# Transposed attention weights gathered into full PSUM banks, and the attention units in another order

## The chip, the cores and the metric

The kernel runs on one core of one Trainium2 chip. The metric is the device time of one execution in microseconds (us); less is better. A figure "of the profile" comes from one execution that was recorded by the hardware profiler. PE is TensorE, ACT ScalarE, DVE VectorE, POOL GpSimd, and SP the engine that issues most of the DMAs.

## What is computed

One encoder layer over 2048 tokens of width 1024, in float32. The mixer has 16 heads of width 64: eight of stick-breaking attention and eight of chunked softmax attention. Cut to what matters here:

```python
mod = silu(c) @ w_ada + b_ada                      # shifts, scales, gates
proj = (rmsnorm(x, g_norm1) * (1 + sc1) + sh1) @ w_in
q_sb, k_sb, v_sb, q_ca, k_ca, v_ca = split(proj)
# stick-breaking: strictly causal
z = q @ k.T * scale
w = where(strict, exp(log_sigmoid(z) + suffix_sum(log_sigmoid(-z))), 0)
o_sb = w @ v
# chunked: own chunk of 64 and 8 before it, learned bias by clipped distance
q, k = rmsnorm(q_ca, g_q), rmsnorm(k_ca, g_k)
o_ca = softmax(q @ k.T * scale + bias) @ v
x = x + gt1 * (concat(o_sb, o_ca) @ w_o)
h = rmsnorm(x, g_norm2) * (1 + sc2) + sh2
x = x + gt2 * (square(relu(h @ w1)) @ w2)
```

## The kernel before

Everything is kept transposed (features on partitions, tokens along the free axis) and the token order is reversed, so that a causal query block looks at key blocks with the same or a higher number. The tokens are cut into NTB = 4 blocks of TB = 512. Products of float32 are made of two parts: `split` (line 138) writes a rounded high part with an ACT copy and the rest as a low part with a DVE subtraction, and a product takes two or three matmuls of these parts.

There are three stages. First come the norm and most of the input projection. Then, from about 420 us of the profile, the attention stage, which the change concerns. Last come the output projection of one token block, the second norm and the MLP, in dense matmuls.

**Units and steps.** The attention stage works through a list `units` (line 1071). A unit is one head, one query block g and, for a stick-breaking unit (class SB, line 756), one key block c; a chunked-softmax unit (class CA, line 820) takes the key blocks g and g + 1 together, and for g = 3 only block 3. There are 80 SB units, 32 of them diagonal (c = g), and 32 CA units. Each unit has STEPS = 4 steps, one for each 128 queries. Step i of the main loop (from line 1149) is the front step of one unit and the back step of the unit LAG = 8 steps, so two units, earlier.

- Front of an SB step: `scores` puts q·k in a PSUM bank `z` (issued one step ahead); `soft1` applies a sigmoid on ACT, a multiplicative scan along the keys on DVE (tile `p`) and a difference on POOL (tile `b`, the weights).
- Front of a CA step: `scores` into `cz` (and, at the unit's first step, the last 128 keys of all four steps into one bank `ct`); `soft1` adds the bias and takes the minimum on DVE; `soft2` makes the exponential on ACT (tile `e`); a DVE reciprocal and a POOL product that scale it follow one step later, in the list `first`.
- Back of a step, in the list `js`: `transposes` (line 727) turns 128x128 blocks of the weights on PE into a PSUM bank `wt`; `parts` (line 735) splits that bank into `wth` (ACT) and `wtl` (DVE); `values` (line 745) multiplies both with the value rows into the accumulator `acc`, at most AVLAG = 3 pieces later.

The piece in which this is done is a key block kb of 128 keys with the queries q0 to q1 that see it. A diagonal SB unit has 4 pieces of 512, 384, 256 and 128 columns. A CA unit with g < 3 has 8 pieces, of 512, 512, 384, 256, 128, 384, 256 and 128 columns, two in each step; with g = 3 it has the 4 of the diagonal. All other SB units have 4 pieces of 512.

**What sets the order.** `z`, `cz`, `ct` and `wt` all come from one pool of 4 PSUM banks (`pz`, line 95) in turn, so PE can begin a new one only when the engines have done with the one four before it. PE keeps program order. Between steps, `fill` (line 1086) adds dense matmuls from a list `filler`: first the remaining input projections (`fill_qkv`, line 949, tiles `pf`), then output projections (`outproj`, line 1000, tiles `po`). A step earns credit in proportion to its unit's weight, one credit pays one matmul of 512 columns, and unspent credit is cut to CAP = 5. After a finished bank of the filler, fill rests until the next step, and at the start of a filler for some steps:

```python
        RESTS = {"wait": 4, "start": 3}
```

An output projection of block g is appended to `filler` when its last pair of heads has been stored (`keep`, line 707): there it is the last CA pair.

ACT holds one set of function tables. The sigmoid of the SB units and the exponential of the CA units stand in different ones, and the compiled program has an ACT_TABLE_LOAD wherever the front goes over from one kind of head to the other. The order of the units before was

```python
        for h in range(NH):
            units += [SB(h, 2, 2), SB(h, 2, 3), SB(h, 3, 3)]
        units += [CA(h, g) for h in range(NH) for g in (2, 3)]
        for g in (1, 0):
            units += [SB(h, g, c) for h in range(NH) for c in range(g, NTB)]
            units += [CA(h, g) for h in range(NH)]
```

so the kind of head changes five times: before units 24, 40, 64, 72 and 104.

Of the kernel before, what the change touches and what calls it, by code (L numbers as in the profile page):

```python
# [18 lines left out]
P = 128  # L19
# [3 lines left out]
NH = 8  # L23
# [56 lines left out]
def encoder_kernel(ctx, tc, xT, c, g1, g2, w_in, w_rest, gqk, bias, w_o, w1, w2, w_ada, b_ada, out):  # L80
# [567 lines left out]
    if True:  # L648
# [67 lines left out]
        pend = {}  # L716

        class Unit:
# [8 lines left out]
            def transposes(self, j):  # L727
                kb, q0, q1 = self.blocks[j]
                nm = f"{self.nm}_{kb}"
                wt = pz.tile([P, TB], F32, tag="z", name=f"wt{nm}")  # L730
                for qi in range(q0, q1):
                    pe.transpose(wt[:, qi * P : (qi + 1) * P], self.weights(qi, kb), ident)
                self.wt[j] = wt

            def parts(self, j):
                kb, q0, q1 = self.blocks[j]
                nm = f"{self.nm}_{kb}"
                wt = self.wt[j]
                wh = wtp.tile([P, TB], F32R, tag="wth", name=f"wth{nm}")
                wl = wtp.tile([P, TB], F32R, tag="wtl", name=f"wtl{nm}")  # L740
                cols = slice(q0 * P, q1 * P)
                split(wh[:, cols], wl[:, cols], wt[:, cols])
                self.wt[j] = (wh, wl, cols, kb)

            def values(self, j):
                if j == 0 and self.first:
                    pend["acc"] = ppo.tile([P, TB], F32, tag="acc", name=f"acc{self.nm}")
                self.acc = pend["acc"]
                wh, wl, cols, kb = self.wt.pop(j)
                end = self.last and j == len(self.blocks) - 1  # L750
                pe.matmul(self.acc[:, cols], self.v[:, kb, :], wh[:, cols], start=self.first and j == 0, stop=False)
                pe.matmul(self.acc[:, cols], self.v[:, kb, :], wl[:, cols], start=False, stop=end)
                if end:
                    soon.append(lambda: finish(self))

        class SB(Unit):
            ca = 0

            def __init__(self, h, g, c):
                self.c = c  # L760
                super().__init__(h, g, c == g, c == NTB - 1)
                self.nm += f"_{c}"
                self.diag = c == g
                self.weight = 0.7 if self.diag else 1.0
                self.blocks = [(kb, 0, kb + 1 if self.diag else 4) for kb in (3, 2, 1, 0)]
# [54 lines left out]
        class CA(Unit):  # L820
            ca = 1

            def __init__(self, h, g):
# [3 lines left out]
                order = [3] + [kb for kb in (4, 2, 1, 0, 5, 6, 7) if kb < self.nk // P]  # L827
                self.blocks = [(kb, max(0, kb - 4), min(4, kb + 1)) for kb in order]
# [257 lines left out]
        def fill(part):  # L1086
# [62 lines left out]
        for i in range(len(steps) + LAG):  # L1149
# [11 lines left out]
            if back is not None:  # L1161
                nb = len(back.blocks)
# [3 lines left out]
            if front is not None:  # L1166
# [15 lines left out]
            fill(front.weight if front else 0.6)  # L1182
# [530 lines left out]
```

## Time and profile before

| | |
|---|---|
| time, median of 3 runs | 2623.31 us (2622.73 to 2624.0) |
| time of the profiled execution | 2620.22 us |
| its span, first to last instruction | 2618.2 us |
| busy: PE, DVE, ACT, POOL | 98%, 72%, 54%, 34% of the span |
| transposes of SB weights (`wt` from `b`) | 1088, from 429.5 to 1242.1 us |
| transposes of CA weights (`wt` from `e`) | 560, from 595.0 to 1317.2 us |
| casts `wth` and subtractions `wtl` | 544 each |
| ACT_TABLE_LOAD | 6, of 1283 ns each |

The table is read so: the span is what the instructions cover, and the time of the same execution is 2.0 us longer. The busy share of PE is of a pipelined engine: the time of one matmul in the profile runs over that of the next, so a busy PE may still be doing less than it could. The `wt` rows show where the attention stage lies, from about 420 to 1318 us. Nearly all rows of the profile carry line 42, since a helper records every operation; the tiles' names tell them apart.

### The profile page before, as it was taken

Reading aid. Unit: us, or ns where it says so; the run is one execution under the profiler, and the core shown is the slowest. Engines: PE = TensorE matmul, PEld = TensorE weight load, DVE = VectorE, ACT = ScalarE, POOL = GpSimd, SP = SyncE. Lnnn points to the kernel's source line nnn. Section 1 sums busy time; section 2 is a strip of 40 time slices with the busy share of each in tenths; the row PEclk is TensorE's granted clock in tenths of the full one; section 3 lists DMA queues with packets and bytes.
Section 4 is the critical chain, followed back from the end, with each engine's and each line's share of the span. In section 5 each row is a group of like instructions: output and inputs, shape, how many; then the busy total and the mean of one; then the engine's idle time right before and its main releaser. Section 6 shows DMA issues by size and latency. Waiting matters only on the chain. (4 is left out here: it accounts for less than half of the span.)

```text
span 2618.2 us, 39617 instructions
## 1 busy us (share of the span) xinstructions
PE 2565.2 (98%) x12816; PEld 2153.3 (82%) x12816; DVE 1881.5 (72%) x3222; ACT 1408.0 (54%) x2704; POOL 896.3 (34%) x1224
## 2 busy tenths in 40 slices
PE   6999999999999999999999999999999999999999
PEld 5888887888789988787888888788888888888887
DVE  7656767887789879898768787668766565555555
ACT  5333434678866676666754444556544454544443
POOL 4330144666666567666604323000002322200000
PEclk9999999999999999999999999999999999999999
DMA  9879977788787688666697777776764434375574
GB/s 344 305 302 363 333 297 252 240 260 260 248 261 226 217 276 262 222 204 209 218 340 249 259 258 277 277 273 231 258 223 173 154 139 166 125 263 195 197 271 151
DMA packets 257039, 640.20 MB, mean 245 GB/s; under 512 B 28736, under 2 KB 60480, under 8 KB 246976
## 3 DMA queue, kind: packets, MB, share of 16 engines
q1 hardware_dynamic: 255536, 632.96, 70.1%
q10 hardware_dynamic: 1296, 4.72, 0.4%
q8 instruction: 101, 1.65, 0.3%
q14 instruction: 106, 0.87, 0.1%
HBM read 446.20 MB, written 191.37 MB: 244 GB/s over the span
## 5 line engine op out<-in xcount | busy, mean ns | idle before, releaser
L42 PE MATMUL ps<-oph,opv 128*128 128x512 f32 x2688 | 614.0, 390 | 1.8 <-ACT opv L42 1.6
L42 PE MATMUL ps<-h,opw 128*128 128x512 f32 x2664 | 604.5, 389 | 0.5 <-DVE cx L42 0.5
L42 PEld LDWEIGHTS ps<-oph,opv 128*128 128x128 f32 x2688 | 505.1, 188 | 108.8 <-ACT opv L42 2.5
L42 PEld LDWEIGHTS ps<-h,opw 128*128 128x128 f32 x2664 | 500.1, 188 | 104.6 <-DVE cx L42 0.9
L42 POOL TENSOR_TENSOR b<-p 128x512 f32<-128x512 f32 (+1 forms) x320 | 291.9, 912 | 219.5 <-DVE p L42 129.6
L42 ACT CAST wth<-wt 128x512 fp32r<-128x512 f32 (+3 forms) x544 | 257.1, 483 | 191.3 <-PE wt L42 180.9
L42 DVE TENSOR_TENSOR wtl<-wt,wth 128x512 fp32r<-128x512 f32 (+3 forms) x544 | 290.6, 545 | 65.0 <-ACT wth L42 62.7
L42 DVE TENSOR_TENSOR oph<-hw,oph 128x512 fp32r<-128x512 f32 x224 | 156.0, 696 | 222.0 <-ACT oph L42 222.0
L42 ACT CAST oph<-hw 128x512 fp32r<-128x512 f32 x224 | 139.3, 622 | 284.9 <-PE ps L42 268.8
L42 PE MATMUL pt<-w,ht 128*128 128x512 f32 x1248 | 288.8, 391 | 2.2 <-DVE qh L42 2.2
L42 PEld LDWEIGHTS pt<-w,ht 128*128 128x128 f32 x1248 | 232.8, 188 | 50.6 <-ACT csq L42 2.9
L42 POOL TENSOR_TENSOR ts<-w 128x512 f32<-128x512 f32 x32 | 46.7, 1460 | 659.5 <-DMA w<-in_w_dram 570.7
L42 DVE TENSOR_TENSOR_SCAN p<-z,p,zero 128x512 f32<-128x512 f32 x192 | 245.6, 1280 | 29.8 <-ACT z L42 24.1
L42 PE MATMUL acc<-wth,v 128*128 128x512 f32 (+3 forms) x544 | 220.9, 410 | 0.2 <-DMA q<-scr_q 0.2
L42 ACT ACTIVATE z<-z 128x512 f32<-128x512 f32 (+1 forms) x320 | 166.2, 520 | 59.0 <-PE z L42 48.6
L42 PE MATMUL z<-k,q 128*128 128x512 f32 (+3 forms) x640 | 184.8, 371 | 8.4 <-DVE p L42 5.9
L42 PE MATMUL acc<-wtl,v 128*128 128x512 f32 (+3 forms) x544 | 185.6, 348 | 0.0
L42 DVE TENSOR_TENSOR opw<-w,opw 128x512 fp32r<-128x512 f32 x127 | 98.8, 780 | 113.2 <-ACT opw L42 113.1
L42 POOL TENSOR_TENSOR e<-e,cols 128x640 f32<-128x640 f32 (+4 forms) x128 | 142.9, 1121 | 104.7 <-DVE cols L42 61.8
L42 PE MATMUL wt<-ident,b 128*128 128x128 f32 x1088 | 171.3, 272 | 2.7 <-DVE cols L42 2.3
L42 PEld LDWEIGHTS wt<-ident,b 128*128 128x128 f32 x1088 | 134.3, 140 | 33.0 <-DVE cols L42 3.5
L42 PE MATMUL po<-fx,ow 128*128 128x512 f32 x576 | 160.3, 393 | 0.0
(190 smaller groups left out, 4069.5 us busy)
## 6 DMA issues: line engine op xcount, KB each, us to landing
hw<-scr_hid SPq DMA_DIRECT2D x112, 512.0 KB, 3.9
q<-scr_q SPq DMA_DIRECT2D x128, 256.0 KB, 4.7
w<-in_w_dram SPq DMA_DIRECT2D x64, 512.0 KB, 5.2
hw<-scr_s SPq DMA_DIRECT2D x64, 512.0 KB, 4.6
k<-scr_k SPq DMA_DIRECT2D x240, 128.0 KB, 4.0
v<-scr_v SPq DMA_DIRECT2D x120, 256.0 KB, 3.9
fw<-scr_w SPq DMA_DIRECT2D x28, 1024.0 KB, 6.1
wa<-in_w_ada_dram SPq DMA_DIRECT2D x48, 512.0 KB, 6.7
```

The lines of the kernel that those rows point to most:

```text
L42: return lambda *x, **y: self.tc.keep_in_program_order(f(*x, **y))
```

## The change

Three things change.

**Banks.** In place of the list of pieces, a unit has a list `banks`, and each bank holds one or two pieces (key block, first and last query, place in the bank). For a diagonal SB unit and a CA unit with g = 3 this is `DIAG`: 512, then 384 + 128, then 256 columns. A CA unit with g < 3 has 512, 512, and three banks of two pieces with 512 columns in all. `transposes` fills the whole bank, `parts` splits the whole bank at once, and `values` still makes two matmuls for each piece, with the same columns as before. So the transposes and the matmuls stay the same in number and size, and the splits go from 544 to 432: three fewer in each of 24 CA units, one fewer in each of 8 CA units with g = 3 and of 32 diagonal SB units. A unit with 3 banks does none in its first back step and one in each other; a unit with 5 does one in each and two in the last.

**Order.** The CA units of g = 1 stand right behind those of g = 2 and 3, and the SB units of g = 1 and g = 0 follow each other, so the kind of head changes three times: before units 24, 48 and 104. An output projection is now appended when all eight pairs of its block are stored, whichever comes last.

**At a change of kind.** In the first step of a unit whose kind differs from the one before (`turned`), `soft1` is issued behind the splits of that step's back unit, and `fill` is given 6 credits more.

```diff
-            if u.ca and u.h == NH - 1 and u.g > 0:
+            pairs[u.g] += 1
+            if pairs[u.g] == KT and u.g > 0:
                 filler.append(Filler(outproj, u.g))
...
             def transposes(self, j):
-                kb, q0, q1 = self.blocks[j]
-                nm = f"{self.nm}_{kb}"
+                nm = f"{self.nm}_{j}"
                 wt = pz.tile([P, TB], F32, tag="z", name=f"wt{nm}")
-                for qi in range(q0, q1):
-                    pe.transpose(wt[:, qi * P : (qi + 1) * P], self.weights(qi, kb), ident)
+                for kb, q0, q1, at in self.banks[j]:
+                    for n, qi in enumerate(range(q0, q1), at):
+                        pe.transpose(wt[:, n * P : (n + 1) * P], self.weights(qi, kb), ident)
                 self.wt[j] = wt
...
-                cols = slice(q0 * P, q1 * P)
-                split(wh[:, cols], wl[:, cols], wt[:, cols])
-                self.wt[j] = (wh, wl, cols, kb)
+                n = P * sum(q1 - q0 for _, q0, q1, _ in self.banks[j])
+                split(wh[:, :n], wl[:, :n], wt[:, :n])
+                self.wt[j] = wh, wl
...
-                pe.matmul(self.acc[:, cols], self.v[:, kb, :], wh[:, cols], start=self.first and j == 0, stop=False)
-                pe.matmul(self.acc[:, cols], self.v[:, kb, :], wl[:, cols], start=False, stop=end)
+                for m, (kb, q0, q1, at) in enumerate(self.banks[j]):
+                    mine = slice(at * P, (at + q1 - q0) * P)
+                    for l in range(2):
+                        pe.matmul(
+                            self.acc[:, q0 * P : q1 * P], self.v[:, kb, :], w[l][:, mine],
+                            start=self.first and j + m + l == 0, stop=end and l == 1 and m == len(self.banks[j]) - 1,
+                        )
...
+        DIAG = [[(3, 0, 4, 0)], [(2, 0, 3, 0), (0, 0, 1, 3)], [(1, 0, 2, 0)]]
...
-                order = [3] + [kb for kb in (4, 2, 1, 0, 5, 6, 7) if kb < self.nk // P]
-                self.blocks = [(kb, max(0, kb - 4), min(4, kb + 1)) for kb in order]
+                if self.nk == TB:
+                    self.banks = DIAG
+                else:
+                    self.banks = [[(3, 0, 4, 0)], [(4, 0, 4, 0)]]
+                    self.banks += [[(kb, 0, kb + 1, 0), (kb + 5, kb + 1, 4, kb + 1)] for kb in (2, 1, 0)]
...
-        for g in (1, 0):
-            units += [SB(h, g, c) for h in range(NH) for c in range(g, NTB)]
-            units += [CA(h, g) for h in range(NH)]
+        units += [CA(h, 1) for h in range(NH)]
+        units += [SB(h, g, c) for g in (1, 0) for h in range(NH) for c in range(g, NTB)]
+        units += [CA(h, 0) for h in range(NH)]
...
-            credit = min(credit, CAP) + part * (work - credit) / (weight * 0.95)
+            credit = min(credit, CAP) + part * (work - credit) / (weight * 0.95) + more
...
+            turned = front is not None and i and front.ca != steps[i - 1][0].ca
-            if front is not None:
+            if front is not None and not turned:
                 front.soft1(fs)
             while first:
                 first.pop(0)()
             for j in js:
                 back.parts(j)
                 late.append((back, j))
+            if turned:
+                front.soft1(fs)
...
-            fill(front.weight if front else 0.6)
+            fill(front.weight if front else 0.6, 6 if turned else 0)
```

How the instructions move is seen at three places. In the rows a name such as `wth_2_2_3` gives head, query block and then, before, the key block of the piece, and after, the number of the bank; the last number is a running one.

The first place is ACT in the CA run, in the four steps in which the unit of head 2, g = 2 is the back unit. Before, it has eight casts, two in each step, between the exponentials `e` of the front unit:

```order
L42 CAST wth_2_2_3_7074<-wt_2_2_3_7057 128x512
L42 CAST wth_2_2_4_7078<-wt_2_2_4_7062 128x512
L42 ACTIVATE e_3_2_0_7082,cols<-s_3_2_0_7067,cols 128x640
L42 CAST wth_2_2_2_7104<-wt_2_2_2_7092 128x384
L42 CAST wth_2_2_1_7108<-wt_2_2_1_7096 128x256
L42 ACTIVATE e_3_2_1_7112,cols<-s_3_2_1_7070,cols 128x640
L42 CAST svf_11_1_7114<-pf_11_1_6700 128x8x64
L42 CAST wth_2_2_0_7148<-wt_2_2_0_7137 128x128
L42 CAST wth_2_2_5_7152<-wt_2_2_5_7139 128x384
L42 ACTIVATE e_3_2_2_7156,cols<-s_3_2_2_7100,cols 128x640
```

Now, in the same place, it has five, all of 512 columns:

```order
L42 CAST wth_2_2_0_6956<-wt_2_2_0_6944 128x512
L42 ACTIVATE e_3_2_0_6960,cols<-s_3_2_0_6949,cols 128x640
L42 COPY otmp_0_2_6717<-acc_1_2_6821 64x512
L42 COPY o_0_2_6716<-acc_1_2_6821 64x512
L42 CAST wth_2_2_1_6980<-wt_2_2_1_6970 128x512
L42 ACTIVATE e_3_2_1_6984,cols<-s_3_2_1_6952,cols 128x640
L42 CAST wth_2_2_2_7015<-wt_2_2_2_7005 128x512
L42 ACTIVATE e_3_2_2_7019,cols<-s_3_2_2_6976,cols 128x640
L42 CAST wth_2_2_3_7042<-wt_2_2_3_7029 128x512
L42 CAST wth_2_2_4_7046<-wt_2_2_4_7034 128x512
L42 ACTIVATE e_3_2_3_7050,cols<-s_3_2_3_7011,cols 128x640
```

One cast stands before each of the first three exponentials, and two before the fourth.

The second place is ACT at the first change from CA to SB heads (the front goes over to head 0, g = 1, key block 1). Before, the table load and the first sigmoid stand ahead of that step's two casts:

```order
L42 ACTIVATE e_7_3_3_8278,cols<-s_7_3_3_8253,cols 128x128
L42 COPY otmp_6_2_8281<-acc_6_2_8115 64x512
L42 COPY o_6_2_8280<-acc_6_2_8115 64x512
L42 ACT_TABLE_LOAD
L42 ACTIVATE z_0_1_1_0_8287<-z_0_1_1_0_8287 128x512
L42 CAST wth_7_2_3_8312<-wt_7_2_3_8294 128x512
L42 CAST wth_7_2_4_8316<-wt_7_2_4_8299 128x512
```

Now the step's one cast stands ahead of the load:

```order
L42 ACTIVATE e_7_1_3_9181,cols<-s_7_1_3_9128,cols 128x640
L42 COPY otmp_4_1_9184<-acc_4_1_9043 64x512
L42 COPY o_4_1_9183<-acc_4_1_9043 64x512
L42 CAST wth_6_1_0_9208<-wt_6_1_0_9201 128x512
L42 ACT_TABLE_LOAD
L42 ACTIVATE z_0_1_1_0_9192<-z_0_1_1_0_9192 128x512
L42 ACTIVATE z_0_1_1_1_9222<-z_0_1_1_1_9222 128x384
```

The split of the step no longer waits for the load, and the sigmoids come behind it.

The third place is PE at the same change, from the step's last value products to the next transposes (x2 and x3 are matmuls in a row). Before:

```order
L42 MATMUL acc_6_3_8284<-wth_6_3_1_8256,v_6_2_7880 128x256
L42 MATMUL acc_6_3_8284<-wtl_6_3_1_8257,v_6_2_7880 128x256
L42 MATMUL z_0_1_1_1_8324<-k_0_1_1_8050,q_0_1_8047 128x384 x2
L42 MATMUL pf_3_1_8243<-fx_2_6696,fw_3_0_7545 128x512 x2
L42 MATMUL wt_7_2_2_8329<-ident,e_7_2_0_8078 128x128
```

Now:

```order
L42 MATMUL acc_5_1_9187<-wtl_5_1_2_9133,v_5_1_8851 128x128
L42 MATMUL z_0_1_1_1_9222<-k_0_1_1_8933,q_0_1_8930 128x384 x2
L42 MATMUL pf_1_1_9153<-fx_2_6570,fw_1_0_8555 128x512 x2
L42 MATMUL pf_1_1_9153<-fx_3_6572,fw_1_0_8555 128x512 x3
L42 MATMUL pf_1_1_9153<-fx_4_6876,fw_1_1_8678 128x512 x3
L42 MATMUL wt_6_1_1_9235<-ident,e_6_1_0_8952 128x128
```

Between the second scores of the new unit and the next transposes stand eight filler matmuls in place of two. At the change before unit 24 there are also some more; at the one before unit 104 there are none either before or now, since the filler list rests there at the start of an output projection.

More of the change, by code (lines that the diff above doesn't have):

```diff
@@ L748, in values @@
                 self.acc = pend["acc"]
-                wh, wl, cols, kb = self.wt.pop(j)
-                end = self.last and j == len(self.blocks) - 1
-                pe.matmul(self.acc[:, cols], self.v[:, kb, :], wh[:, cols], start=self.first and j == 0, stop=False)
-                pe.matmul(self.acc[:, cols], self.v[:, kb, :], wl[:, cols], start=False, stop=end)
+                w = self.wt.pop(j)
+                end = self.last and j == len(self.banks) - 1
+                for m, (kb, q0, q1, at) in enumerate(self.banks[j]):
[5 more added lines that the diff above has]
+                        )
                 if end:
                     soon.append(lambda: finish(self))
+        DIAG = [[(3, 0, 4, 0)], [(2, 0, 3, 0), (0, 0, 1, 3)], [(1, 0, 2, 0)]]
         class SB(Unit):
@@ L764, in __init__ @@
                 self.weight = 0.7 if self.diag else 1.0
-                self.blocks = [(kb, 0, kb + 1 if self.diag else 4) for kb in (3, 2, 1, 0)]
+                if self.diag:
+                    self.banks = DIAG
+                else:
+                    self.banks = [[(kb, 0, 4, 0)] for kb in (3, 2, 1, 0)]
             def load(self):
@@ L1084, in encoder_kernel, with fill @@
         late, soon, first = [], [], []
-        def fill(part):
+        def fill(part, more=0):
             nonlocal credit, rest, work, weight
-            credit = min(credit, CAP) + part * (work - credit) / (weight * 0.95)
+            credit = min(credit, CAP) + part * (work - credit) / (weight * 0.95) + more
             weight -= part
@@ L1161, in encoder_kernel @@
             if back is not None:
-                nb = len(back.blocks)
+                nb = len(back.banks)
                 js = range(nb * bs // STEPS, nb * (bs + 1) // STEPS)
```

6 lines of the change are left out of this document (4 added, 2 removed).

## The prediction

> **What bounds the kernel now.** I read the page first. Its span, its first list and one of its groups of instructions:
>
> ```profile
> span 2618.2 us, 39617 instructions
> PE 2565.2 (98%) x12816; PEld 2153.3 (82%) x12816; DVE 1881.5 (72%) x3222; ACT 1408.0 (54%) x2704; POOL 896.3 (34%) x1224
> L42 PE MATMUL ps<-h,opw 128*128 128x512 f32 x2664 | 604.5, 389 | 0.5 <-DVE cx L42 0.5
> ```
>
> PE is the bound: it is idle for 53.0 us of the span. No matmul or transpose is taken away by the change, so it can win only what PE waits inside the attention stage. The next view is busy time by windows, cut where the kind of head changes (width, then PE, weight loads, DVE, ACT, POOL, granted clock, DMA share, GB/s):
>
> ```profile
> 435.00:580.00 145.00, 142.82 (x854) 122.72 (x853) 122.47 (x180) 99.86 (x210) 95.47 (x181) 1.00 0.79 242
> 580.00:600.00 20.00, 19.25 (x139) 17.97 (x138) 15.41 (x55) 16.09 (x36) 10.31 (x10) 1.00 1.03 292
> 600.00:705.00 105.00, 99.48 (x636) 87.55 (x636) 75.69 (x285) 86.25 (x217) 66.84 (x66) 0.98 0.82 256
> 705.00:722.00 17.00, 13.44 (x74) 10.89 (x72) 9.57 (x27) 12.19 (x29) 8.70 (x15) 0.90 0.71 203
> 722.00:893.00 171.00, 170.68 (x1085) 151.73 (x1084) 155.06 (x194) 111.90 (x216) 109.69 (x192) 1.00 0.74 235
> 893.00:905.00 12.00, 11.58 (x84) 10.72 (x84) 8.88 (x33) 8.46 (x17) 5.59 (x5) 1.00 0.89 263
> 905.00:970.00 65.00, 63.83 (x419) 56.38 (x418) 50.73 (x183) 49.81 (x118) 39.13 (x32) 1.00 0.87 271
> 970.00:995.00 25.00, 23.43 (x140) 19.52 (x140) 18.98 (x34) 19.50 (x42) 15.71 (x24) 1.00 0.85 282
> 1084.00:1100.00 16.00, 13.05 (x73) 10.11 (x72) 12.34 (x17) 8.73 (x17) 10.24 (x20) 1.00 0.64 199
> 1222.00:1242.00 20.00, 17.49 (x104) 13.93 (x103) 15.09 (x49) 12.07 (x24) 11.80 (x15) 1.00 0.62 187
> 1350.00:1650.00 300.00, 300.00 (x1326) 248.38 (x1325) 242.46 (x329) 146.06 (x256) 98.94 (x62) 1.00 0.76 272
> ```
>
> Width less PE gives the idle time: 5.52 us in the run of chunked-softmax (CA) units of g = 2 and 3 (600:705), 3.56 where it ends (705:722), 0.75, 0.42 and 1.57 at the first, third and fourth change (580:600, 893:905, 970:995), 1.17 in the CA units of g = 1, 2.18 among the first stick-breaking (SB) units, 2.95 and 2.51 at 1084 and 1222. Two windows also lose clock: 0.02 of 105 is 2.1 us, 0.10 of 17 is 1.7. The last row, from the MLP where PE never rests, gives the price of a matmul of 512 columns: 300 / 1326 = 226 ns from start to start. One is shown as 389 ns long, so each wait hides another 0.16 us behind the modelled end.
>
> Then the waits of PE in the two worst windows (total, times, longest), first 600:705, then 705:722:
>
> ```profile
> PE cz L42 <- DVE wtl L42: 2.7, 2, 2.0
> PE cz L42 <- DVE cols L42: 2.1, 3, 0.9
> PE wt L42 <- DVE cols L42: 0.6, 1, 0.6
> ```
>
> ```profile
> PE wt L42 <- DVE cols L42: 2.3, 1, 2.3
> PE z L42 <- DVE cols L42: 1.2, 1, 1.2
> ```
>
> PE waits to begin a score bank or a bank of transposes, and DVE ends the wait: the pool of four PSUM banks is full, because DVE, itself behind ACT, has not read one out. Nowhere in these windows does PE wait for a load.
>
> **The change part by part.** *Fewer splits.* The casts and the subtractions by size:
>
> ```profile
> L42 ACT CAST wth<-wt 128x512 fp32r<-128x512 f32 x280 | 163.4, 587 | 122.0 <-PE wt L42 119.1 <-PE acc L42 0.3
> L42 ACT CAST wth<-wt 128x384 fp32r<-128x384 f32 x88 | 42.3, 480 | 33.7 <-PE wt L42 27.4 <-PE acc L42 6.0
> L42 ACT CAST wth<-wt 128x256 fp32r<-128x256 f32 x88 | 32.8, 373 | 15.5 <-PE wt L42 14.9
> L42 ACT CAST wth<-wt 128x128 fp32r<-128x128 f32 x88 | 23.4, 265 | 20.2 <-PE wt L42 19.5
> L42 DVE TENSOR_TENSOR wtl<-wt,wth 128x512 fp32r<-128x512 f32 x280 | 186.4, 672 | 21.8 <-ACT wth L42 20.9
> L42 DVE TENSOR_TENSOR wtl<-wt,wth 128x384 fp32r<-128x384 f32 x88 | 47.9, 544 | 12.7 <-ACT wth L42 12.5
> L42 DVE TENSOR_TENSOR wtl<-wt,wth 128x256 fp32r<-128x256 f32 x88 | 36.1, 410 | 26.0 <-ACT wth L42 25.9
> L42 DVE TENSOR_TENSOR wtl<-wt,wth 128x128 fp32r<-128x128 f32 x88 | 24.4, 277 | 4.5 <-ACT wth L42 3.3
> ```
>
> 384 + 128 columns in one go save 480 + 265 - 587 = 158 ns of ACT and 544 + 277 - 672 = 149 ns of DVE; 256 + 256 save 159 and 148. Over 112 merges that is 17.7 us of ACT and 16.6 us of DVE, most of it under PE's own work. On the path it counts where PE waits for these engines. In 600:705 there are eight pairs of CA units with four merges each: 32 x 0.158 = 5.1 us of ACT (busy 86.25 of 105), and each step but the unit's last now asks for one bank of transposes where it asked for two, out of four. PE loses 5.52 + 2.1 us there; I take 5.0 as won, with bounds of 0 (the waits sit where nothing was merged) and 7.6. In 905:970 and 435:580 the same merges stand against 1.17 + 2.18 = 3.35 us; I take 1.5 (0 to 3.35), since in the SB units only one merge in a diagonal unit helps.
>
> *Fewer changes of kind.* ACT around the second change, and what PE does then:
>
> ```profile
> 710.06 0.58 ACT L42 COPY o<-acc 64x512 f32<-64x512 f32 x1
> 710.66 1.28 ACT L42 ACT_TABLE_LOAD   x1
> 711.95 0.58 ACT L42 ACTIVATE z<-z 128x512 f32<-128x512 f32 x1
> 712.44 0.59 ACT L42 CAST wth<-wt 128x512 fp32r<-128x512 f32 x1
> ```
>
> ```profile
> 709.10 1.04 PE L42 MATMUL wt<-ident,e 128*128 128x128 f32 x8
> 710.91 0.64 PE L42 MATMUL pf<-fx,fw 128*128 128x512 f32 x2
> 713.84 0.33 PE L42 MATMUL wt<-ident,e 128*128 128x128 f32 x1 [2.29 <-DVE cols L42]
> ```
>
> The load holds ACT for 1.3 us from the copy's end to the next sigmoid, and the casts stand behind it, so no bank comes free and PE runs out of work for 2.29 us. Two of five changes go. Their windows, 893:905 and 970:995, lose 0.42 + 1.57 = 2.0 us; I take all of it (bounds 0 and 2.0). The Trainium skill, page "ScalarE: Activation LUTs", section "What ACT_TABLE_LOAD costs", puts a switch at 1283 ns and about 1380 ns of drain, 2.66 us; the trace agrees with the 1283 and shows no drain (710.64 to 710.66). By the page two removed switches would free an estimated 5.3 us and the sum below would be up to 3.3 us better; by the rows they free 2.6.
>
> *At a change.* The one remaining change from CA to SB has its cast ahead of the load, and eight filler matmuls in place of two. The chain there is cast, load, sigmoid and scan, the last from its row:
>
> ```profile
> L42 DVE TENSOR_TENSOR_SCAN p<-z,p,zero 128x512 f32<-128x512 f32 x192 | 245.6, 1280 | 29.8 <-ACT z L42 24.1 <-POOL p L42 5.0
> ```
>
> 0.59 + 1.29 + 0.58 + 1.28 = 3.7 us, against PE work of some 3.5 us by the order: value products 0.45, scores 0.34, fillers 8 x 0.226 = 1.8, four transposes 0.5 (eight take 1.04) and value products 0.45. Of the 2.29 us about 0.2 stays; the wait of 1.17 us ahead of the load in the same window has another cause and stays too. So 3.56 + 1.7 becomes 1.4: 3.9 won (bounds 0 and 5.3). The first change, with more fillers as well, wins 0.5 of its 0.75. The last change wins nothing: its filler rests before and now, and the norm's wait in its window (2.51) remains.
>
> The clock goes with the long waits here: 0.90 in the window with the 2.29 us gap, 0.98 in the one with a gap of 2.0. The Trainium skill, page "TensorE: Matmul & The Clock Gate", section "HAM oscillation", asks for "no PE-idle gaps >~3.4µs", and these are shorter. By that rule the lost clock has another cause and stays, and the sum would be 3.8 us less, 8.0; the trace speaks against it.
>
> *Waits that go* also take the 0.16 us each that the rows hide: about 13 waits, 2.1 us (0 to 4).
>
> *What is late next.* The work by step becomes uneven: a CA unit splits one bank in three steps and two in the fourth, a diagonal unit none in its first. And by the order the filler now rests over five steps, not four, at the start of its second output projection (the window at 1084), one of them with only two score matmuls, 0.45 us, against a scan of 1.28. I charge 1.0 for that and two or three waits of the mean size in 600:705, 5.4 / 6 = 0.9 us, for the uneven steps: 3.2 (0 to 20, the third rival).
>
> *Loads.* The CA units of g = 1 come 24 units earlier with their DMAs, and the projections they need (288 credits) are through by unit 30. Value tiles have two buffers, so SP waits with such a load, and what is queued behind it, until PE has done; in 905:990:
>
> ```profile
> SPq L685 <- PE acc L42: 18.2, 7, 4.5
> ```
>
> A bank's products now trail by three banks, about a step longer, so these waits grow by some 2 us each. They are covered by the steps between a load and its use; all waits of PE for a load in the attention stage come to this:
>
> ```profile
> PE acc L42 <- DMA q<-scr_q: 0.2, 1, 0.2
> ```
>
> I cost them at nothing; without that cover it would be up to 2 us for each of eight units.
>
> *Sum*: 5.0 + 1.5 + 2.0 + 3.9 + 0.5 + 2.1 - 3.2 = 11.8 us. The profiled execution took 2620.2 us, 2.0 more than its span, and the median of the runs is 3.1 above it. So the profiled time becomes 2608.4 and the median 2611.5 us.
>
> **The rivals.** *More goes than I take.* If every wait up to 995 us goes, that is 5.52 + 3.56 + 0.75 + 0.42 + 1.17 + 1.57 + 2.18 = 15.2, 3.8 of clock and some 20 times 0.16: 22 us, 2601. For it: the pool of banks is the cause in nearly all of them. Against it: DVE stays at 155 of 171 us busy in the SB window 722:893.
>
> *The splits were covered.* PE waits for the last of several things, and ACT is idle 19 us and DVE 29 us in 600:705; if their spare time moves with the casts, only the changes pay: 2.0 + 3.9 + 0.5 + 0.7 (four waits' hidden ends) - 3.2 = 3.9, 2619.4: no change that can be told.
>
> *Slower: the double step.* In the last back step of each of 24 CA units two banks of transposes, the next scores and the next `ct` want all four banks at once, and the following unit's first steps come too thin to make up for it. If PE waits 0.9 us at each, that is 21.6 in place of the 2.2 charged: the sum falls to -7.6 and the time is 2631. It breaks even at 13 such waits more than charged and is slower by over 0.2% from 19. Against it: before, each step had this pressure, and there were six waits in 16 units.
>
> *The change doesn't do what it says*: the order shows 432 casts and three table loads in the attention stage, so only the credit at the last change is without effect; that is in the sum.
>
> **How the numbers follow.** About 0.2%, 5.2 us, is what a measurement of this kernel can tell from no change: below 2618.1 is faster, above 2628.5 slower. The forecast, 2606 to 2617, has 0.58; more won 0.12; splits covered 0.20, of which 0.03 still comes out as faster; the double step 0.08; no effect at all 0.02. So 0.73 faster, 0.19 the same, 0.08 slower. For 8 in 10 the range takes in the forecast with its bounds, half of the larger gain and most of the covered case: 2603.5 to 2620.5.
>
> **What would show it.** Right: 432 casts and as many subtractions; three table loads in the attention stage; no wait of over 1 us of PE right behind the load that ends the CA run; idle time in that run's windows under half of before; a clock of 1.00 around it; DVE and ACT each about 17 us less busy. Wrong: PE idle as long as before in the attention stage with the same count of waits (covered), or many waits of PE for `wtl` in each fourth step of the CA units (double step), or waits of PE for loads of `v`.

## The result and the profile after

The changed kernel takes 2609.78 us in the median of four runs (2605.65 to 2612.98); the kernel before, run beside it, 2623.65 (2622.73 to 2624.71). The ratio is 0.9946 with a 95% interval of 0.9929 to 0.9963: 13.9 us less. The forecast was 2611.5. The profiled execution is the slowest of the four, 2612.98 us.

The page of the changed kernel, span and engines:

```profile
span 2611.0 us, 39248 instructions
PE 2563.8 (98%) x12816; PEld 2152.3 (82%) x12816; DVE 1875.8 (72%) x3110; ACT 1392.8 (53%) x2590; POOL 895.6 (34%) x1224
```

PE has the same 12816 matmuls; DVE and ACT have 112 and 114 instructions fewer. The splits by size and the table loads, now:

```profile
L42 ACT CAST wth<-wt 128x512 fp32r<-128x512 f32 x392 | 229.1, 586 | 170.1 <-PE wt L42 165.8 <-DVE wtl L42 0.7 <-DMA q<-scr_q 0.5
L42 ACT CAST wth<-wt 128x256 fp32r<-128x256 f32 x40 | 14.9, 372 | 12.3 <-PE wt L42 12.0
L42 DVE TENSOR_TENSOR wtl<-wt,wth 128x512 fp32r<-128x512 f32 x392 | 263.7, 677 | 55.8 <-ACT wth L42 54.4
L42 DVE TENSOR_TENSOR wtl<-wt,wth 128x256 fp32r<-128x256 f32 x40 | 16.3, 408 | 3.4 <-ACT wth L42 3.1
L42 ACT ACT_TABLE_LOAD x4 | 5.1, 1283 | 4.3 <-DVE cols L42 3.6 <-PEq L1718 0.7
```

392 + 40 = 432 of each. The four groups of casts of before come to 261.9 us, these two to 244.0; the subtractions go from 294.8 to 280.0. The table loads go from six to four. So the change does what its text says.

Busy time by windows, cut where the kind of head changes (columns as in the prediction). The last row lies in the MLP:

```profile
435.00:577.00 142.00, 141.65 (x861) 123.71 (x862) 122.93 (x167) 97.59 (x198) 96.87 (x185) 1.00 0.82 249
577.00:602.00 25.00, 23.15 (x160) 20.90 (x159) 18.11 (x64) 19.36 (x42) 12.53 (x12) 1.00 0.83 261
602.00:705.00 103.00, 100.57 (x651) 88.75 (x650) 75.54 (x269) 85.83 (x199) 70.00 (x69) 1.00 0.87 269
705.00:778.00 73.00, 73.00 (x457) 63.94 (x456) 54.89 (x190) 58.66 (x122) 46.83 (x38) 1.00 0.92 281
778.00:804.00 26.00, 26.00 (x171) 23.26 (x171) 21.21 (x30) 19.88 (x37) 16.13 (x26) 1.00 0.78 267
804.00:1060.00 256.00, 254.60 (x1575) 223.05 (x1575) 231.30 (x281) 163.98 (x308) 168.13 (x290) 1.00 0.76 239
1060.00:1085.00 25.00, 22.02 (x120) 17.26 (x119) 20.70 (x25) 13.74 (x25) 16.07 (x32) 1.00 0.78 254
1207.00:1230.00 23.00, 18.23 (x98) 14.26 (x97) 14.53 (x46) 11.07 (x23) 11.34 (x14) 0.93 0.50 163
1670.00:1690.00 20.00, 15.12 (x58) 12.00 (x57) 10.07 (x16) 7.85 (x14) 0.00 (x0) 0.83 0.78 264
```

Width less PE, as before: the first SB units (435:577) lose 0.35 us where they lost 2.18. The first change (577:602) loses 1.85, before 0.75. The CA run loses 2.43 in 602:705 at full clock, before 5.52 and 2.1 of clock. The CA units of g = 1 (705:778) and the change out of the run (778:804) lose nothing; before, these places lost 0.42 + 1.17 + 1.57 and 3.56 + 1.7. But the last change (1207:1230) loses 4.77 and 0.07 x 23 = 1.6 of clock, before 2.51 and none, and the SB run (804:1060) loses 1.40, where its two parts (722:893 and 995:1084) lost 0.32 and nothing.

At the change out of the CA run, ACT and then PE in the changed kernel (start, length, engine, operation):

```profile
781.17 0.58 ACT L42 CAST wth<-wt 128x512 fp32r<-128x512 f32 x1
781.77 1.28 ACT L42 ACT_TABLE_LOAD   x1
783.07 0.96 ACT L42 ACTIVATE z<-z 128x512 f32<-128x512 f32 x2
```

```profile
781.35 2.01 PE L42 MATMUL pf<-fx,fw 128*128 128x512 f32 x8
783.20 0.60 PE L42 MATMUL wt<-ident,e 128*128 128x128 f32 x4
784.96 0.66 PE L42 MATMUL wt<-ident,e 128*128 128x128 f32 x4
```

The cast stands ahead of the load, the eight filler matmuls run beside the load, and PE begins the next transposes with no wait noted at the row's end, where 2.29 us stood.

The last transposes of the attention stage start at 1304.2 us; they started at 1317.3. That is 13.1 us earlier, but the span is only 7.2 shorter, since this execution loses more in the MLP. The place that answers there to the last row above, in the kernel before:

```profile
1690.00:1710.00 20.00, 18.28 (x73) 14.43 (x72) 15.44 (x25) 12.96 (x25) 0.00 (x0) 0.91 1.03 390
```

After: 4.88 idle and 0.17 x 20 = 3.4 of clock; before: 1.72 and 1.8. That is 4.8 us of the 5.9 by which the gain shrinks; the rest I did not trace. ACT waits about 7 us there for a load of `hw` in both kernels, and the change does not touch that code.

### The profile page after: what moved, and what is told of

It is laid out like the page before. It is cut to its first block, busy times and chain, and to the rows that moved or that the text cites. A ratio compares the mean times of both kernels' runs of the same rounds, so it can differ in the third digit from the quotient of the medians.

```text
span 2611.0 us, 39248 instructions
## 1 busy us (share of the span) xinstructions
PE 2563.8 (98%) x12816; PEld 2152.3 (82%) x12816; DVE 1875.8 (72%) x3110; ACT 1392.8 (53%) x2590; POOL 895.6 (34%) x1224
## 5 line engine op out<-in xcount | busy, mean ns | idle before, releaser
L42 ACT CAST wth<-wt 128x512 fp32r<-128x512 f32 (+1 forms) x432 | 244.0, 566 | 182.4 <-PE wt L42 177.8
L42 DVE TENSOR_TENSOR wtl<-wt,wth 128x512 fp32r<-128x512 f32 (+1 forms) x432 | 280.0, 652 | 59.2 <-ACT wth L42 57.5
L42 DVE TENSOR_TENSOR_SCAN p<-z,p,zero 128x512 f32<-128x512 f32 x192 | 245.8, 1281 | 28.8 <-ACT z L42 20.6
```

The costliest lines, as they stand in the source:

```text
L42: return lambda *x, **y: self.tc.keep_in_program_order(f(*x, **y))
```

## The experiments

The theory behind the forecast: PE lost time because splits held the four PSUM banks, most of all in the CA run and at the change out of it; the merges, the order and the treatment of a change each pay, in different places. The rivals: the merges were covered and only the changes pay; or uneven steps eat the gain. The runs came in three sets of four, each kernel against the kernel before on the same chip; the medians of the kernel before were 2623.31, 2623.57 and 2622.46 us in the three sets. All results first (us; median, range, number of runs; the ratio to the kernel before has its 95% interval):

| kernel | median | range, runs | ratio |
|---|---|---|---|
| banks only | 2610.84 | 2607.44 to 2620.35, 6 | 0.9953 (0.9937 to 0.9968) |
| order only | 2619.56 | 2612.83 to 2623.37, 12 | 0.9982 (0.9974 to 0.9991) |
| banks and order | 2611.71 | 2611.18 to 2613.02, 5 | 0.9953 (0.9941 to 0.9965) |
| treatment only | 2618.67 | 2614.98 to 2620.95, 11 | 0.9984 (0.9975 to 0.9992) |
| after, `os` in four buffers | 2609.88 | 2608.12 to 2612.47, 5 | 0.9950 (0.9935 to 0.9964) |
| before, `os` in four buffers | 2618.94 | 2616.16 to 2624.66, 12 | 0.9982 (0.9972 to 0.9992) |
| after, splits first only toward SB | 2609.47 | 2607.40 to 2611.41, 6 | 0.9948 (0.9934 to 0.9962) |
| after, no credit | 2614.12 | 2608.46 to 2614.81, 6 | 0.9962 (0.9948 to 0.9976) |
| banks only, `os` in four buffers | 2606.82 | 2603.33 to 2609.77, 5 | 0.9940 (0.9928 to 0.9953) |
| banks of the CA units only | 2616.35 | 2612.66 to 2625.75, 11 | 0.9978 (0.9968 to 0.9988) |
| banks of diagonal units only | 2630.77 | 2625.02 to 2633.80, 6 | 1.0032 (1.0020 to 1.0043) |
| after, rest ahead of the change | 2605.45 | 2605.31 to 2606.93, 5 | 0.9937 (0.9925 to 0.9950) |

To place the gains, one more number is worked out from each trace: the time that PE loses. It is the distance from each start of a PE instruction to the next, less the median distance for the same shape over all traces, summed over a stretch. It takes in the waits, the clock, and the ends that the rows only model. It is of one execution of each kernel, and executions of one kernel differ by up to 13 us here, so small differences in this table prove nothing alone. The stretches: from the first transpose of an SB weight to the first of a CA weight ("first"), from there to the 240th transpose of a CA weight, which ends the CA units of g = 2 and 3 ("run"), and from there to the last ("rest").

| kernel | first | run | rest |
|---|---|---|---|
| before | 9.8 | 16.4 | 23.3 |
| before, `os` in four buffers | 9.0 | 11.2 | 25.0 |
| order only | 9.5 | 9.5 | 23.0 |
| treatment only | 10.2 | 8.7 | 24.9 |
| banks of the CA units only | 9.9 | 8.7 | 21.2 |
| banks of diagonal units only | 5.7 | 30.3 | 23.7 |
| banks only | 5.8 | 10.0 | 20.7 |
| banks only, `os` in four buffers | 5.6 | 7.7 | 20.6 |
| banks and order | 5.4 | 10.2 | 21.3 |
| after | 6.2 | 5.6 | 24.0 |
| after, `os` in four buffers | 6.5 | 5.6 | 22.7 |
| after, splits first only toward SB | 5.3 | 5.6 | 21.9 |
| after, no credit | 8.8 | 7.2 | 21.2 |
| after, rest ahead of the change | 3.1 | 8.4 | 22.5 |

**The parts one by one.** Full banks alone: the order and the treatment of before.

```diff
-        units += [CA(h, 1) for h in range(NH)]
-        units += [SB(h, g, c) for g in (1, 0) for h in range(NH) for c in range(g, NTB)]
-        units += [CA(h, 0) for h in range(NH)]
+        for g in (1, 0):
+            units += [SB(h, g, c) for h in range(NH) for c in range(g, NTB)]
+            units += [CA(h, g) for h in range(NH)]
...
-            turned = front is not None and i and front.ca != steps[i - 1][0].ca
+            turned = False
```

> Full banks (432 splits), but the units in the order of before (five changes of kind) and no special treatment at a change. My theory after the result, that full banks are the main part: the waits among the first SB units and in the CA run go (about 4 + 5 + 2 us by the profile of the changed kernel), so 9 to 11 us faster than before, 2613 to 2615 us. Rival, that the changes of kind are the main part: 2 to 4 us faster, 2620 to 2622 us, with the long waits at the five table loads as before.

2610.84 us, about 12.3 less than before by the ratio: nearly the whole gain. The change out of the CA run has the code of before, and still it loses only 1.62 us, at full clock, where 3.56 and 1.7 of clock stood:

```profile
705.00:731.00 26.00, 24.38 (x141) 20.55 (x141) 21.30 (x34) 19.91 (x42) 16.69 (x28) 1.00 0.81 253
```

The order alone: one piece in each bank, 544 splits, no treatment.

```diff
-        DIAG = [[(3, 0, 4, 0)], [(2, 0, 3, 0), (0, 0, 1, 3)], [(1, 0, 2, 0)]]
+        DIAG = [[(kb, 0, kb + 1, 0)] for kb in (3, 2, 1, 0)]
...
-                    self.banks = [[(3, 0, 4, 0)], [(4, 0, 4, 0)]]
-                    self.banks += [[(kb, 0, kb + 1, 0), (kb + 5, kb + 1, 4, kb + 1)] for kb in (2, 1, 0)]
+                    self.banks = [[(kb, max(0, kb - 4), min(4, kb + 1), 0)] for kb in (3, 4, 2, 1, 0, 5, 6, 7)]
...
-            turned = front is not None and i and front.ca != steps[i - 1][0].ca
+            turned = False
```

> Only the order with three changes of kind; splits of 512, 384, 256 and 128 columns as before (544), no special treatment at a change. My theory: the two windows that go lost 2.9 us with the hidden ends of their waits, so 2 to 3 us faster than before, about 2621 us. Rival, that the changes of kind are the main part: 6 us or more faster, 2617.5 us or less.

2619.56 us, about 4.7 less by the ratio, 3.8 by the medians. "Rest", where two changes went and the exit of the CA run came in, goes from 23.3 to 23.0, and "run" from 16.4 to 9.5. Part of that is the exit that now lies elsewhere, but not all: in 600:705, where the units stand in the order of before, this kernel loses 4.31 us at full clock against 5.52 and 2.1 of clock.

Banks and order without the treatment (`turned = False` alone):

> The changed kernel without the special treatment at a change (scans and sigmoids stand ahead of the splits, no credits added). By my forecast the treatment is worth 4.4 us (3.9 at the change to SB heads and 0.5 at the first), so 2614 us. Rival: it wins there and loses as much at the last change, where no filler comes, so 2609 to 2611 us, as the changed kernel.

2611.71 us, the same as banks alone. On top of full banks, the order wins nothing that can be measured in these runs. This kernel's trace has a long wait of its own, of 4.4 us, to which the next part comes.

The treatment alone: one piece in each bank and the old order, by the same lines as above, with `turned` left as in the change.

> Only the special treatment at a change, in the order of before with its five changes, and 544 splits. By my forecast's price of 3.9 us for a change to SB heads, and of 0.5 for a change to CA heads: 4 to 6 us faster than before, 2618 to 2620 us. Rival: the treatment costs at the changes where no filler comes what it wins at the others, 2622 to 2625 us.

2618.67 us, about 4.2 less by the ratio. The three parts alone come to 12.3 + 4.7 + 4.2 = 21 us, together they win 14: they take away some of the same waits. And two quite different edits alone both took 7 to 8 us out of "run", where neither touches the size of the splits. Something else was being moved there.

**A store that ACT waits for.** ACT in the CA run of the kernel before, then PE at that time:

```profile
639.02 0.19 ACT L42 ACTIVATION_READ_ACCUMULATOR e<-s,cols 128x1 f32 x1
642.25 0.62 ACT L42 CAST os<-o 128x512 fp32r<-128x512 f32 x1 [3.04 <-DMA scr_m<-os]
```

```profile
643.65 1.22 PE L42 MATMUL cz<-k,q 128*128 128x512 f32 x2 [1.97 <-DVE wtl L42]
```

`os` (line 709) has a single buffer. Its cast stands in ACT's program order, and here it waits 3.04 us until the store of the previous `os` has landed. The casts `wth` stand behind it, DVE waits for them, and PE, whose row names only DVE, waits 1.97 us for a bank. The second row is also at half clock: two matmuls in 1.22 us. So the largest wait in this window, which the forecast laid to the splits, had its root in a store. The next runs take `os` from another tile's pool and give that pool four buffers in place of three:

```diff
-            os = op.tile([P, 2, TB], F32R, tag="os", name=f"os{u.nm}", bufs=1)
+            os = fp.tile([P, 2, TB], F32R, tag="st", name=f"os{u.nm}")
...
-        fp = ph.enter_context(tc.tile_pool(name="fp", bufs=3))
+        fp = ph.enter_context(tc.tile_pool(name="fp", bufs=4))
```

In the changed kernel:

> The changed kernel, with the tile os (the split head outputs on their way to memory) taken from the pool of four staging tiles instead of having one buffer of its own. In the profile of the changed kernel no ACT instruction of the attention stage waits over 0.6 us for a store of os; so if that profile is typical, no difference, 2608 to 2611 us. Rival: the wait comes in some executions and makes their spread (2605.7 to 2613.0), then 2606 to 2608 us and a spread of 3 us at most.

2609.88 us: nothing. Its ACT waits for that store only 0.5 us in all.

In the kernel before:

> The kernel before, with os from the pool of four staging tiles. Its profile has ACT waiting 3.0 us at 642 us and 1.3 us at 482 us for a store of os, and PE idle for 2.0 us behind the first, with 1.7 us of clock lost after it. If these waits are typical, and not covered: 3 to 5 us faster than before, 2618.5 to 2620.5 us, and that much of what full banks win is this wait. Rival: they are covered by what else is late, 2622 to 2624 us.

2618.94 us: 4.6 less, and "run" falls from 16.4 to 11.2. So about a third of what the change wins was a wait for a store that it moved out of the way. In all, ACT waits for this store 4.3 us in the kernel before, 2.8 with the order alone, 0.7 with the treatment alone and 0.5 in the changed kernel, but 5.2 with banks and order, of which 4.4 in one wait: in these traces each edit moves it, and not always for the better.

**The parts of the treatment.** `soft1` behind the splits only where the front goes over to SB heads:

```diff
-            if front is not None and not turned:
+            if front is not None and not (turned and not front.ca):
...
-            if turned:
+            if turned and not front.ca:
```

> The changed kernel, with the splits ahead of the scans only at the change to SB heads; at the two changes to CA heads the order is as before. The changed kernel loses 7.7 us of PE around the last change, where the kernels without the treatment lose 4.0. If the order of the splits there is the cause: about 3 us faster than the changed kernel, 2606 to 2607.5 us. Rival, that it is the execution (a clock drop of 1.7 us and a late load): no difference, 2608 to 2611 us.

2609.47 us, as the changed kernel: at the two changes to CA heads, the place of `soft1` makes no difference that can be measured. And without the six credits (`fill(front.weight if front else 0.6, 0)`):

> The changed kernel without the 6 credits at a change; the splits still stand ahead of the scans. By my forecast the eight fillers cover most of the 2.3 us at the change to SB heads, and the cast ahead of the load alone less than half of it: 1 to 2 us slower than the changed kernel, 2611 to 2612 us. Rival: with full banks the pool holds through the table load anyway, no difference, 2608 to 2611 us.

2614.12 us; the intervals overlap, so the 4.3 us are not certain. The trace cannot place them: its execution took 2608.46 us, the fastest of the six. It does show one difference: "first" goes from 6.2 to 8.8. PE's waits in the window of the first change (575 to 602 us) of this kernel:

```profile
PE cz L42 <- DVE wtl L42: 2.7, 1, 2.7
PE wt L42 <- DVE cols L42: 0.2, 1, 0.2
```

One wait of 2.7 us, and 0.06 x 27 = 1.6 us of clock with it, where the changed kernel's longest wait is the 0.8 us for a load. But with banks and order and no treatment at all, the longest wait there is 1.5 us and "first" is 5.4: the credits make good what `soft1` behind the splits costs at this change, and hardly more.

**Which merges pay.** Full banks with the old order, no treatment and `os` in four buffers:

> Full banks in the order of before, without the treatment at a change, and os from the pool of four staging tiles. If full banks and the waits for the store of os are two causes: 12.3 + 4.6 us, about 2606.5 us. If full banks win in part because the stores are less in ACT's way: no more than full banks alone, 2609 to 2611 us.

2606.82 us, 15.6 less than before. Here the two nearly add: 12.3 + 4.6 = 16.9. With `os` out of the way on both sides, the merges are worth 15.6 - 4.6 = 11.0 us, each against the kernel before of its own set, and the whole change 2618.94 - 2609.88 = 9.1. So order and treatment together win nothing that can be measured beside full banks and a free `os`. Merges in CA units only (the diagonal SB units keep four pieces; old order, no treatment):

```diff
-                    self.banks = DIAG
+                    self.banks = [[(kb, 0, kb + 1, 0)] for kb in (3, 2, 1, 0)]
```

The line stands in the SB unit.

> Full banks in the CA units only (24 units with five banks and 8 with three, 80 of the 112 merges); the diagonal SB units keep four splits. Order of before, no treatment at a change. By the shares of my forecast (5.0 for the CA run, 0.8 of the 1.5 behind it): 8 to 10 of the 12.3 us that full banks win, 2613 to 2615 us. Rival, that the first SB units win as much (their windows lost 8.1 us and lose 5.5): 5 to 6 us, 2617.5 to 2618.5 us.

2616.35 us, 6.1 less than before, near the rival's 5 to 6 and not the 8 to 10 by the forecast's shares: "first" stays at 9.9, as it must, and "run" is 8.7. Merges in the diagonal units only, that is 32 in SB units and 8 in CA units of g = 3; the other CA units keep their eight pieces:

> Full banks in the 32 diagonal SB units and the 8 CA units with g = 3 only (40 of the 112 merges); the other CA units keep eight splits. Order of before, no treatment at a change. By my forecast at most 2 us faster than before, 2621 to 2623.5 us. Rival: as much as the CA units, 5 to 6 us faster, 2617.5 to 2618.5 us.

2630.77 us: slower than before, with the whole interval above 1. Neither theory had that. "First" is 5.7, as good as with all banks; the loss lies in "run". Its window, ACT in it, and the waits of the window:

```profile
599.00:718.00 119.00, 103.17 (x636) 90.48 (x634) 74.69 (x275) 85.44 (x210) 67.61 (x66) 0.94 0.74 232
```

```profile
673.66 0.20 ACT L42 ACTIVATION_READ_ACCUMULATOR e<-s,cols 128x1 f32 x1
681.46 0.62 ACT L42 CAST os<-o 128x512 fp32r<-128x512 f32 x1 [7.61 <-DMA scr_m<-os]
```

```profile
PE cz L42 <- DVE wtl L42: 11.4, 3, 7.5
ACT os L42 <- DMA scr_m<-os: 11.3, 3, 7.6
```

ACT waits 11.3 us in three waits for stores of `os`, PE 11.4 us in three waits behind it, and the clock falls to 0.94 over 119 us, 7 us more. Of this kernel's stores, the slowest took 7.9 us to land:

```profile
DMA to landing us min/median/max: 2.6/3.0/7.9
```

It is the same wait as in the kernel before, only longer. This is read from the trace: a kernel with these banks and `os` in four buffers was not run. Why that store took 7.9 us stays open.

**A version with all of it.** The changed kernel with `os` in four buffers, `soft1` behind the splits only toward SB heads, and the filler spread a little differently, so that its rest at the start of the last output projection comes ahead of the last change:

```diff
-            credit = min(credit, CAP) + part * (work - credit) / (weight * 0.95) + more
+            credit = min(credit, CAP) + part * (work - credit) / (weight * 0.9) + more
```

> A version meant to be faster: the changed kernel with os from the pool of four staging tiles, the splits ahead of the scans only at the change to SB heads, and the filler's pace set from 0.95 to 0.9, so that its rest before the last output projection ends where the last change begins and seven and nine fillers follow there. If the rest at the last change is what costs there (5.6 to 7.7 us lost in its window, of which 2.3 are the norm's): 3 us faster than the changed kernel, 2606 to 2607 us. Rival: the rest costs as much wherever it stands, 2609 to 2611 us.

2605.45 us, the lowest median of all, within 1.6 us over its five runs. Its interval overlaps that of the changed kernel, so that it is faster is not shown. PE at the last change in the changed kernel (waits in 1207 to 1230 us), then the window of the last change in this version:

```profile
PE wt L42 <- DVE cols L42: 2.5, 2, 2.1
PE cz L42 <- DVE wtl L42: 1.8, 1, 1.8
PE wt L42 <- DVE wtl L42: 0.5, 1, 0.5
```

```profile
1213.00:1239.00 26.00, 23.54 (x133) 19.14 (x132) 18.45 (x64) 14.90 (x30) 12.25 (x14) 1.00 0.56 157
```

Idle 2.46 us at full clock in place of 4.77 and 1.6. At the first change it has no idle time at all, as its window shows:

```profile
575.00:602.00 27.00, 27.00 (x196) 25.14 (x195) 19.75 (x69) 20.02 (x44) 14.01 (x15) 1.00 0.84 242
```

## Why the prediction was right, point by point

The time came out 1.7 us from the forecast, and the main part of the mechanism is borne out: full banks alone bring 12.3 us. That the sum is so close is in part luck, since several of its terms were wrong and their errors cancelled. One thing stays open: a merge frees a bank and also saves about 158 ns of ACT and 149 of DVE, and no run separates the two. A kernel that fills the banks but still splits each piece by itself would.

- **The CA run, 5.0.** In 600:705 idle time and clock fell by 5.2 us, as the sum had it. But 1.97 us of that idle time and some 1.8 of the clock hung on the store of `os`, not on splits. The step that failed is "DVE, itself behind ACT, has not read one out": true, but it stopped at ACT and did not ask what ACT waited for. The merges alone, with `os` free on both sides, bring "run" from 11.2 to 7.7: 3.5, and some of that lies at its exit. In the window itself the idle time falls only from 3.80 to 3.30 us. (For the run's units with g = 3 the forecast also had one bank too many: they asked for one in each step, not two.) The window without the merges, then with them, both with `os` free:

```profile
600.00:705.00 105.00, 101.20 (x655) 88.72 (x653) 78.00 (x291) 89.57 (x226) 70.31 (x68) 1.00 0.85 266
600.00:705.00 105.00, 101.70 (x665) 90.53 (x664) 76.71 (x271) 89.14 (x202) 72.27 (x70) 1.00 0.84 265
```

- **Merges elsewhere, 1.5.** Too small. In the kernels with full diagonal banks "first" lies at 5.3 to 6.5, but for the 8.8 without credit and the 3.1 of the last version, and at 9.0 to 10.2 in all with single pieces: about 4 us from one merge in each diagonal SB unit. The forecast capped this by the idle time in the window, 2.18; "lost" also counts the modelled ends. "Rest" falls with the merges alone as well, by 2.6 us, or by 4.4 with `os` free.
- **Two removed changes, 2.0, and the change out of the run, 3.9.** The idle time went as said, and 3.56 + 1.7 became 0, not 1.4. But the 3.9 counts again what the merges win: with full banks alone the change out of the run already loses only 1.62, so the treatment had at most that left to win there, not 3.9. What the two removed changes won did not reach the total, and where it went is open but for the wait for a load of `k` shown below: banks and order take as long as banks alone, and beside full banks and a free `os`, order and treatment win nothing that can be measured. The forecast also charged nothing for what they give back: in the changed kernel's trace the first change and the last one are dearer.
- **The first change, 0.5.** It lost 1.1 instead, of which 0.8 is a wait for a load of `fw`. By these traces the treatment brings nothing there: "first" is 5.4 with banks and order alone and 6.2 in the changed kernel.
- **The last change, 0.** It lost 3.9 more. The filler rests there before and after, as the forecast read from the order; but its last matmuls before the rest now run at 1206 us and the next at 1220. The waits are the kernel's: with `os` in four buffers they are the same, but the clock stays at 1.00, so the 1.6 of clock is this execution's. In 1200:1245 PE is idle for 2.55 us with banks and order but no treatment, about as before (2.51); for 3.93 with `soft1` behind the splits and no credit; for 4.17 with the credits and `soft1` in its old place; and for 4.77 with both. So both parts of the treatment cost there. In the last version, which has the rest ahead of the change, the window loses 2.46.
- **Uneven steps and the longer rest, -3.2.** The rest at the second output projection costs what it did: 2.98 in 1060:1085, 2.95 before. PE's waits that are left in the CA run (602 to 705 us) of the changed kernel:

```profile
PE wt L42 <- DVE cols L42: 0.9, 2, 0.6
PE wt L42 <- DVE wtl L42: 0.8, 2, 0.4
PE ct L42 <- DVE cols L42: 0.7, 2, 0.4
```

  Six short waits, 2.4 us, in 16 units, near the 2.2 charged: the "double step" did not come.
- **Loads, 0.** Right for the changed kernel. With banks and order alone one wait for a load of `k` appears in PE's waits, so the cover is thin:

```profile
PE ct L42 <- DMA k<-scr_k: 1.5, 1, 1.5
```

- **Busy time.** ACT is 15.2 us less busy, near the 17 forecast. DVE is only 5.7 less: its subtractions fell by 14.8, but other groups grew, such as the sums over `w2s` in the MLP, from 65.5 to 69.0, where the change touches nothing.

The rival "splits covered" falls with the banks alone. "More goes" was not reached: with all the changes of the last version the time is 2605.45, and its 2601 stayed out of reach.

## What to carry to other kernels

Fill a PSUM bank before evacuating it: here one wide split in place of two narrow ones left PE the same 12816 matmuls and took one bank fewer each time, and that alone was worth nearly the whole of this change. A term for a place where two parts of a change both act should be priced with the other part already in: here one part had taken most of what the other was to win. When the row of a waiting engine names a second engine, follow that engine back too, to the end of the chain; here it led to a store with one staging buffer, whose wait stood in the program order of a shared engine. Gains from edits that relieve the same place do not add, and where each edit moves the timing of such a store, an edit can look good, or (by its trace) bad by 8 us, for a reason that is not its own.

## What the runs showed of the chip

The clock. Two windows of the kernel before, around the two long waits:

```profile
636.00:647.00 11.00, 8.71 (x47) 7.60 (x48) 5.67 (x26) 6.84 (x18) 7.40 (x8) 0.84 0.68 221
712.00:720.00 8.00, 6.06 (x28) 5.04 (x29) 5.64 (x10) 4.51 (x11) 3.21 (x7) 0.79 0.69 175
```

Each loses 0.16 x 11 or 0.21 x 8 us, about 1.7: the clock record shows one stretch of 3.4 us at half rate in each, after waits of 1.97 and 2.29 us. The rows at 1084 and 1222 in the prediction show idle time of 2.5 to 3 us in several waits, and a clock of 1.00. The last change shows the same wait with and without that loss: behind 1.76 us at 1216 us the changed kernel runs at half rate, and behind 1.77 us at the same place its version with `os` in four buffers does not.

```profile
1216.01 1.22 PE L42 MATMUL cz<-k,q 128*128 128x512 f32 x2 [1.76 <-DVE wtl L42]
1216.84 0.73 PE L42 MATMUL cz<-k,q 128*128 128x512 f32 x2 [1.77 <-DVE wtl L42]
```

So a wait near 2 us sometimes costs another 1.7 us, and this is part of why runs of one kernel differ: among the four of the changed kernel the mean granted clock goes from 0.997 in the slowest (2612.98 us) to 1.000 in the fastest (2605.65), and 0.003 of 2611 us is 7.8. The Trainium skill, page "TensorE: Matmul & The Clock Gate", section "What's actually happening", has the clock judged by a free-running window of 4096 cycles at 1.2 GHz, 3413 ns; the length of the stretches agrees with that, and a window that does not start with the wait could be why only some waits are hit. The rule "no PE-idle gaps >~3.4µs" in the same page's section "HAM oscillation" is not strict enough here: shorter gaps cost clock.

The store. The 31 stores of `os` that SP issues, all of 512 KB, take 2.6 to 7.9 us to land in the slower kernel above, with a median of 3.0. With one buffer ACT waited for the slow ones, up to 7.61 us.
